# Splitting the first x load of a batched matmul into two transfers of half rows

## The chip, the cores and the metric

The kernel runs on one core of a Trainium2 chip. The metric is the device time of one execution in microseconds (us), taken as the median of several runs. All runs are "fast" (none is more than 1.5% above the fastest run of its kernel). A ratio of two kernels is the mean time of one kernel's fast runs over that of the other's of the same rounds, with a 95% interval, so it is not quite the ratio of the medians that are quoted beside it. "Same" means within 2%.

## The reference

```python
batch, m, k, n = 16, 512, 768, 1024        # float32 throughout
def reference(x, y):                       # x: (16, 768, 512), y: (16, 768, 1024)
    return np.einsum('bkm,bkn->bmn', x, y).astype(np.float32)
```

It is sixteen independent products. For each batch element 1.57 MB of x and 3.15 MB of y come in, and 2.10 MB go out. Together this is 109 MB.

## The kernel before

SyncE issues all transfers, in the order of the program. VectorE casts x and y to bf16, TensorE multiplies, and ScalarE copies PSUM to the output buffers. There are two buffers each for x and y in float32, two for each in bf16 and five for the output. A partition holds 6 neighbouring rows of k, so its part of x is one contiguous run of 12 KB in DRAM, and its part of y one of 24 KB.

The helper `wide_dma` on its first call with a key issues a plain transfer; every later call copies that instruction with a DRAM side whose rows are joined, four partitions' worth to a row for x and two for y. Both then read 48 KB at a time: the trace of the kernel before has 1440 packets of 49,152 bytes.

```python
def wide_dma(key, dst, src, dram_rows, load):
    if key not in made:
        made[key] = nc.sync.dma_start(dst, src)       # first call: plain
        return made[key]
    ...                                               # later calls: a copy with joined DRAM rows

def load(b):
    i = b % 2
    if b >= 2:
        nc.sync.wait_ge(cast, nx[b - 2])              # until the buffer of x is cast
    wide_dma("x", xs[i][:], x_v[b], 4, True).then_inc(sx[i], 16)
    if b >= 2:
        nc.sync.wait_ge(cast, nx[b - 2] + parts(b - 2))
    wide_dma("y", ys[i][:], y_v[b], 2, True).then_inc(sy[i], 16)
...
for b in range(B):                                    # VectorE
    i = b % 2
    n = 16 * (b // 2 + 1)
    if b >= 2:
        nc.vector.wait_ge(groups, 2 * (b - 1))
    nc.vector.wait_ge(sx[i], n)
    nc.vector.tensor_copy(xb[:, i], xs[i][:]).then_inc(cast, 1)
    nc.vector.wait_ge(sy[i], n)
    ...                                               # the cast of y
```

## Time and profile before

| what | before |
|---|---|
| time, median of the 3 runs | 260.69 us (260.46 to 260.75) |
| span of the profile | 259.0 us |
| busiest compute engine | PE, 69% |
| share of the 16 DMA engines on q1 | 98.5% |
| first cast of x, first cast of y | 7.14 us, 15.05 us |
| cast of the second y | 26.04 us |

The page is read from the DMA rows down, and not from the engines. A packet is one DMA record of the trace, and the page counts the share of the 16 DMA engines from these records. In the kernel before, queue q1 has 3744 packets of 12 to 48 KB, and 768 records of 4 bytes, which is 16 for each of the 48 transfers. These are called semaphore writes here, as the trace has just as many semaphore updates that came from transfers (768); the page counts them as packets too. The compute engines have gaps; the transfers have none to speak of but at the ends (in the DMA row, 7 tenths in the first slice, 5 in the last, and 8 or 9 in all others). The landings of the loads can be read at the casts that wait for them. The cast of y is the better mark of the two, as it always waits for its transfer in the first part of the kernel (the first seven end 3.6 to 6.1 us of idle time of VectorE, each released by the transfer).

### The profile page before, as it was taken

To read this page: it belongs to the slowest core of one execution; us is meant where nothing else is said; L and a number is where in the kernel's file an instruction comes from. 1 tells how busy PE (TensorE), PEld (TensorE's weight loads), DVE (VectorE), ACT (ScalarE), POOL (GpSimd) and SP (SyncE) were. 2 spreads that over 40 slices of the span, in tenths; PEclk is the share of its full clock that TensorE was granted. 3 is DMA by queue.
4 is the path that set the end of the run, shared out by engine and by line. 5 is a ranking of instruction groups with operands and counts; after the bars stand their busy time and mean duration, and the time that the engine had idled before them with its cause. 6 is when DMAs were issued, how large, how long until landed. Compare 5 with 4: busy or idle time off the path is not lost. (4 is left out here: it accounts for less than half of the span.)

```text
span 259.0 us, 2506 instructions
## 1 busy us (share of the span) xinstructions
PE 179.0 (69%) x768; PEld 88.9 (34%) x768; DVE 82.0 (32%) x33; ACT 60.9 (24%) x33; POOL 0.2 (0%) x4
## 2 busy tenths in 40 slices
PE   0009999999999006999069999595008999969500
PEld 0004555554545002454025555252003555534200
DVE  0261645527164350002245263300242536410000
ACT  1000342244220005222202241433000234052300
POOL 0000000000000000000000000000000000000000
PEclk9999999999999855899759999999555999988965
DMA  7999989899999999999999998999999999999995
GB/s 270 428 490 395 471 380 478 380 471 395 456 402 448 387 428 425 433 463 456 410 440 410 440 448 377 435 423 463 471 387 471 395 456 410 395 428 438 423 435 240
DMA packets 4514, 109.07 MB, mean 421 GB/s; under 512 B 768, under 2 KB 768, under 8 KB 768
## 3 DMA queue, kind: packets, MB, share of 16 engines
q1 hardware_dynamic: 4512, 109.05, 98.5%
q14 instruction: 2, 0.02, 0.0%
HBM read 75.50 MB, written 33.55 MB: 421 GB/s over the span
## 5 line engine op out<-in xcount | busy, mean ns | idle before, releaser
L154 PE MATMUL ps<-yb,xb 128*128 x768 | 179.0, 397 | 64.3 <-PEq L149 64.3
L154 PEld LDWEIGHTS ps<-yb,xb 128*128 x768 | 88.9, 116 | 154.0 <-issue 82.6
L170 ACT COPY ob<-ps 128x2048 f32<-128x2048 f32 x32 | 59.6, 1872 | 179.0 <-PE ps L154 139.9
L132 DVE CAST yb<-ys 128x6144 bf16<-128x6144 f32 (+1 forms) x17 | 53.8, 3171 | 77.2 <-DMA ys<-in_y_dram 77.2
L128 DVE CAST xb<-xs 128x3072 bf16<-128x3072 f32 x16 | 28.2, 1760 | 68.3 <-DMA xs<-in_x_dram 53.7
L170 ACT ACT_TABLE_LOAD x1 | 1.3, 1283 | 5.3 <-issue 5.3
L200 POOL MEMSET const-bfloat16-1.0<- 128x1 bf16 x1 | 0.1, 103 | 0.0
L200 POOL MEMSET const-uint8-127<- 128x1 uint8 x1 | 0.1, 103 | 0.0
L200 POOL MEMSET const-float32-0.0<- 128x1 f32 x1 | 0.1, 99 | 0.2 <-issue 0.2
L200 POOL MEMSET const-float32-1.0<- 128x1 f32 x1 | 0.1, 99 | 0.0
## 6 DMA issues: line engine op xcount, KB each, us to landing
ys<-in_y_dram SPq DMA_DIRECT2D x16, 3072.0 KB, 18.6
out_dram<-ob SPq DMA_DIRECT2D x16, 2048.0 KB, 26.3
xs<-in_x_dram SPq DMA_DIRECT2D x16, 1536.0 KB, 20.1
```

The source lines that it names most:

```text
L128: nc.vector.tensor_copy(xb[:, i], xs[i][:]).then_inc(cast, 1)
L132: nc.vector.tensor_copy(yb[:, i, ks], ys[i][:, ks]).then_inc(cast, 1)
L154: mm = nc.tensor.matmul(ps[g][:, m, nt], x_w[:, bass.ds(s, 1), kt, mo], yb[:, bass.ds(s, 1), kt, nt * NF:(nt + 1) * NF], start=(kt == 0), ...
L170: cp = nc.scalar.copy(ob[b % NO][:, g * HB:(g + 1) * HB].rearrange("p m (t f) -> p m t f", f=NF), ps[g][:])
L200: nc = _bacc.Bacc("TRN2", target_bir_lowering=False, num_devices=1)
```

## The change

The diff has no visible purpose but the start: the first x comes as two transfers, each of half of every partition's row, so that packets at the start are of 6 KB and not of 12. It asks for both halves before the cast.

```diff
+    XF = 2
...
-        wide_dma("x", xs[i][:], x_v[b], 4, True).then_inc(sx[i], 16)
+        if b == 0:
+            for k in range(0, KT, KT // XF):
+                ks = slice(k, k + KT // XF)
+                nc.sync.dma_start(xs[0][:, ks], x_v[0, :, ks]).then_inc(sx[0], 16)
+        else:
+            wide_dma("x", xs[i][:], x_v[b], 4, True).then_inc(sx[i], 16)
...
-        nc.vector.wait_ge(sx[i], n)
+        nc.vector.wait_ge(sx[i], n + 16 * (XF - 1) * (i == 0))
```

## The prediction

> **What bounds the kernel now.** I read the whole-program page first, then the time line of the start, then windows over single stretches of the transfers, then the waits of the DMA queue. From the page before:
>
> ```profile
> span 259.0 us, 2506 instructions
> PE 179.0 (69%) x768; PEld 88.9 (34%) x768; DVE 82.0 (32%) x33; ACT 60.9 (24%) x33; POOL 0.2 (0%) x4
> ...
> DMA  7999989899999999999999998999999999999995
> GB/s 270 428 490 395 471 380 478 380 471 395 456 402 448 387 428 425 433 463 456 410 440 410 440 448 377 435 423 463 471 387 471 395 456 410 395 428 438 423 435 240
> DMA packets 4514, 109.07 MB, mean 421 GB/s; under 512 B 768, under 2 KB 768, under 8 KB 768
> ...
> q1 hardware_dynamic: 4512, 109.05, 98.5%
> ```
>
> The reader is to see that no compute engine is above 69%, while the transfers hold the 16 DMA engines for 98.5% of the span and show a gap only in the first and the last slice. The bytes are fixed: 75.50 MB in and 33.55 MB out by the page. So this is a DMA-bound kernel, and a change can win time only by starting the stream of transfers earlier, by making its packets cheaper, or by shortening the tail after it. The chain of work that ended last names PE with only 5% of the span, because it breaks off at the last matmuls; I don't use it.
>
> The start, from the time line before (start, duration, engine, line, operation):
>
> ```profile
> 0.95 0.39 SPq L74 DMA_DIRECT2D xs<-in_x_dram  x1
> 1.39 0.42 SPq L74 DMA_DIRECT2D ys<-in_y_dram  x1
> 1.86 0.54 SPq L74 DMA_DIRECT2D xs<-in_x_dram  x1
> 2.44 0.65 SPq L74 DMA_DIRECT2D ys<-in_y_dram  x1
> 5.34 1.28 ACT L170 ACT_TABLE_LOAD   x1 [5.34 <-issue]
> 7.14 1.76 DVE L128 CAST xb<-xs 128x3072 bf16<-128x3072 f32 x1 [7.14 <-DMA xs<-in_x_dram]
> 8.93 0.47 SPq L74 DMA_DIRECT2D xs<-in_x_dram  x1
> 15.05 3.36 DVE L132 CAST yb<-ys 128x6144 bf16<-128x6144 f32 x1 [6.14 <-DMA ys<-in_y_dram]
> ```
>
> All four first loads are issued by 3.09 us. The first x is cast from 7.14 to 8.90 us, and then VectorE sits idle for 6.14 us until the first y lands at 15.05. TensorE needs both, so the landing of the first x has about 6 us of slack. An earlier or later first x alone is worth nothing.
>
> Windows over the start, in which the columns after the length are the busy time of five engines, the granted clock, the DMA share and the GB/s (a packet is counted with its whole time and size in the window in which it starts):
>
> ```profile
> 1.75:2.25 0.50, 0.00 (x0) 0.00 (x0) 0.00 (x0) 0.00 (x0) 0.00 (x0) 1.00 1.38 246
> 3.50:6.00 2.50, 0.00 (x0) 0.00 (x0) 0.00 (x0) 0.66 (x1) 0.00 (x0) 1.00 0.98 418
> 8.00:12.00 4.00, 0.00 (x0) 0.00 (x0) 0.90 (x1) 0.00 (x0) 0.00 (x0) 1.00 0.99 422
> 16.00:26.00 10.00, 7.01 (x23) 3.03 (x24) 4.17 (x2) 0.00 (x0) 0.00 (x0) 1.00 0.92 398
> 1.75:257.25 255.50, 178.96 (x768) 88.86 (x768) 81.99 (x33) 60.89 (x33) 0.00 (x0) 0.88 1.00 427
> ```
>
> The last line is the model I use: the stream begins at about 1.75 us, its last packets start by 257.25, and in between the engines' share is 1.00 at 427 GB/s. The other lines give the time of one packet, as share x length x 16 engines / number of packets, where the number is rate x length / packet size. First x, packets of 12,288 B: 0.98 x 2.5 x 16 = 39.2 us over 418 x 2.5 / 12.288 = 85 packets, 0.461 us each. First y, 24,576 B: 63.4 us over 68.7, 0.922 us. Later loads, 49,152 B: 147.2 us over 81.0, 1.818 us. Four packets of 12 KB cost 1.844 us where one of 48 KB costs 1.818, so each of the three additional packets costs about 0.009 us (estimate; the shares have two digits, so it may be 0 to 0.015). The very first packets: 1.38 x 0.5 x 16 = 11.0 us over 246 x 0.5 / 12.288 = 10 packets, 1.10 us each, which is 0.64 more than a packet in the stream.
>
> [...]
>
> **The change part by part.**
> 1. One more issue on the DMA queue, about 0.4 us by the rows above. The first y is then issued at about 1.8 instead of 1.39, the last of the first loads ends at about 3.5. The engines have the 1.57 MB of x to move until about 6.5 us, so the queue behind it is full in time. On the path: 0.
> 2. The first x: 128 packets of 12 KB become 256 of 6 KB, for each engine 16 instead of 8. The bytes are the same. Added: 8 x 0.009 = 0.07 us, all on the path, because the engines have no idle time to hide it in. One more semaphore write for each engine: about 0.01.
> 3. A part that the diff hides: the helper makes a plain transfer on the first call with each key, and copies it in its wide form afterwards. The first x no longer goes through the helper, so the second x is now its first call and comes plain: 12 KB packets instead of 48 KB, for each engine 8 packets instead of 2. Added: 6 x 0.009 = 0.05 us, on the path too.
> 4. The wait of the cast on both halves (32 instead of 16, and all later waits on that semaphore 16 higher) starts nothing early: no half is used alone. The order of instructions on every engine is otherwise the same, by a comparison of the two built programs. Time: 0.
> 5. The start of the stream. The first packets take 0.64 us more than the others. If this is latency alone, a shorter packet doesn't change when the second one flows: 0.
>
> Sum: 0.07 + 0.01 + 0.05 = 0.13 us longer, so 260.69 + 0.13 = 260.8 us. Nothing downstream amplifies it: by the waits of the DMA queue below, SyncE waits for casts for the buffers long before the queue runs dry, so a shift of 0.1 us shifts the stream and no more.
>
> ```profile
> SPq L74 <- DVE yb L132: 96.2, 12, 9.0
> SPq L74 <- DVE xb L128: 69.1, 12, 26.0
> ```
>
> **The rivals.** (a) A shorter ramp. [...]the first packet costs one packet's time extra, and with 6 KB this is 0.46 / 2 = 0.23 us less. For it speaks that 1.10 us is not far from twice 0.461 us; against it that one cannot tell it from plain latency. Net of the 0.13 us it makes 260.6 us. It may well be the intent of the change. (b) The transfers of half rows are dearer than I take them: the source of a half is 6 KB of every 12 KB, and the halves or the plain second x could leave the 16 engines more unequal, or the packets could be cut at 2 KB if the rows of the slice are not merged. Then an engine has 48 packets for the first x instead of 8, 40 x 0.009 = 0.36 us more, 261.1 to 261.2 us. Against it: in the kernel before only the 768 semaphore writes are under 8 KB, so the same three-dimensional form was merged to whole rows. (c) The earlier first half lets compute start early and the gain runs through: impossible here, since both halves are waited for and the first y lands some 6 us after the cast of x. This makes 0. (d) The phase between loads and TensorE changes, and a wait for buffers stops the stream. In the first phase a pair of loads takes 10.99 us, by the landings of y at 15.05 and 26.04, and a stop of a microsecond would need the queue to be several microseconds poorer than it is; I give it one chance in twenty and up to a microsecond either way.
>
> **Range and chances.** The sum is smaller than what repeated runs differ by (260.46 to 260.75), so the verdict can only be the same. Between (a) at 260.6 and (b) at 261.2 I add about 0.4 us on each side for the runs and (d): 260.2 to 261.5, centre 260.8. Two per cent is 5.2 us, forty times the sum; I give each side one chance in a hundred.
>
> **What would show it.** In the profile after: 4514 + 128 + 96 + 16 = 4754 packets; those under 8 KB 768 + 256 + 16 = 1040; a q1 share still at 98% or 99%; the first cast of x within 0.3 us of 7.14, that of y within 0.3 us of 15.05 and the second x as a plain load. If the start of the first y cast is earlier by some 0.2 us, and the span with it, rival (a) is right and step 5 is wrong. If there are some 512 packets more under 8 KB, the rows were not merged. A span that differs by over 1 us, or a slice in the middle with a DMA share of 7 or less that was not there before, would make the prediction wrong.

The 0.01 us of a semaphore write has no source in the prediction; the 768 records of 4 bytes in the trace of the kernel before have a median of 0.009 us. That the first packet costs one packet's time extra, in rival (a), is an assumption with the size of a measured packet (0.46 us).

## The result, and the profile after

The changed kernel took 260.68 us (260.51 to 260.75, 4 runs) against 260.72 us (260.46 to 260.76, 4 runs). The ratio is 1.000, with an interval from 0.9982 to 1.0017: "same". The output is correct.

The page of the changed kernel, with the rows that answer to those of before:

```profile
span 258.7 us, 2507 instructions
PE 176.9 (68%) x768; PEld 88.4 (34%) x768; DVE 82.0 (32%) x33; ACT 60.9 (24%) x33; POOL 0.2 (0%) x4
...
DMA  7999999999999999999999999999999999999996
DMA packets 4754, 109.07 MB, mean 422 GB/s; under 512 B 784, under 2 KB 784, under 8 KB 1040
...
q1 hardware_dynamic: 4752, 109.06, 98.6%
```

There is one instruction more, and 240 packets more. Those under 8 KB grew from 768 to 1040, which is the 256 packets of 6 KB and 16 semaphore writes. The DMA row is as full as before (q1 98.6%, before 98.5%).

The start of the changed kernel, from its time line (start, duration, engine, line, operation):

```profile
0.95 0.86 SPq L113 DMA_DIRECT2D xs<-in_x_dram  x2
1.86 0.43 SPq L75 DMA_DIRECT2D ys<-in_y_dram  x1
2.33 0.68 SPq L75 DMA_DIRECT2D xs<-in_x_dram  x1
3.05 0.53 SPq L75 DMA_DIRECT2D ys<-in_y_dram  x1
...
7.38 1.76 DVE L136 CAST xb<-xs 128x3072 bf16<-128x3072 f32 x1 [7.38 <-DMA xs<-in_x_dram]
...
14.99 3.36 DVE L140 CAST yb<-ys 128x6144 bf16<-128x6144 f32 x1 [5.85 <-DMA ys<-in_y_dram]
```

The two halves are issued back to back in 0.86 us, and the other three first loads move back by about half a microsecond. The first x lands 0.24 us later than in the profile of before, and the first y 0.06 us earlier. The cast of the first y still ends an idle time of VectorE of almost 6 us. The second y is cast at 25.98 us here and at 26.04 before. Whether the 0.24 us belongs to the change, only a second profile of the same kernel can tell; it is the first experiment.

### The profile page after: what moved, and what is told of

Same layout as the page of the kernel before. It is cut to its first block, busy times and chain, and to the rows that moved or that the text cites. A ratio compares the mean times of both kernels' runs of the same rounds, so it can differ in the third digit from the quotient of the medians.

```text
span 258.7 us, 2507 instructions
## 1 busy us (share of the span) xinstructions
PE 176.9 (68%) x768; PEld 88.4 (34%) x768; DVE 82.0 (32%) x33; ACT 60.9 (24%) x33; POOL 0.2 (0%) x4
## 2 busy tenths in 40 slices
DMA packets 4754, 109.07 MB, mean 422 GB/s; under 512 B 784, under 2 KB 784, under 8 KB 1040
## 3 DMA queue, kind: packets, MB, share of 16 engines
q1 hardware_dynamic: 4752, 109.06, 98.6%
## 5 line engine op out<-in xcount | busy, mean ns | idle before, releaser
L162 PE MATMUL ps<-yb,xb 128*128 x768 | 176.9, 394 | 65.7 <-PEq L157 65.7
```

Of the source, the lines that this page charges most:

```text
L162: mm = nc.tensor.matmul(ps[g][:, m, nt], x_w[:, bass.ds(s, 1), kt, mo], yb[:, bass.ds(s, 1), kt, nt * NF:(nt + 1) * NF], start=(kt == 0), ...
```

## The experiments

The theory is that the time is the start of the stream of transfers plus the sum of its packets, since the DMA engines never run dry (q1 has 98.5% of their time in the kernel before) and nothing downstream is on the path. The rivals are that smaller first packets shorten the ramp, that half rows are dear for the memory, and that an earlier or later start of compute runs through to the end.

### Both kernels once more

The edit is none.

> The kernel before once more, to learn what two profiles of one and the same kernel differ by. All theories: 260.7 us, ratio 1.000. The start of the stream (first packets), the first cast of x (7.14 us in the first profile) and that of y (15.05) should come back within 0.05 us if the changed kernel's later first x (7.38) is due to the change, and move by 0.1 to 0.3 us if it is the noise of one execution.

> The changed kernel once more, five rounds. Theory (a stream that is never empty, 0.009 us for each additional packet): 260.8 us, ratio about 1.0005. Rival (smaller first packets shorten the ramp by 0.23 us): 260.6 us, ratio about 0.9996. First cast of x at 7.38 again if its delay belongs to the change, first cast of y at 15.0.

In the same rounds the kernel before took 260.82 us (9 runs). Its copy took 260.81 us, ratio 0.9999 (0.9986 to 1.0013). The changed kernel took 260.80 us, ratio 0.9996 (0.9982 to 1.0009). The casts in the new profile of the kernel before:

```profile
7.54 1.76 DVE L128 CAST xb<-xs 128x3072 bf16<-128x3072 f32 x1 [7.54 <-DMA xs<-in_x_dram]
...
14.93 3.36 DVE L132 CAST yb<-ys 128x6144 bf16<-128x6144 f32 x1 [5.62 <-DMA ys<-in_y_dram]
```

One and the same kernel casts its first x at 7.14 in one execution and at 7.54 in another. The changed kernel's 7.38 (and 7.46 in its new profile) lies between, so its later first x says nothing about the change. The marks further on are steadier. The second y is cast at 26.04 and 25.93 us in the two profiles of before, and at 25.98 and 25.93 in the two of after. So the change is not seen at the second y within about 0.1 us. The added 0.13 us of the prediction is neither shown nor excluded by this.

### The halves alone, without the plain second x

```diff
         wide_dma("y", ys[i][:], y_v[b], 2, True).then_inc(sy[i], 16)
+        made.setdefault("x", made["y"])      # changed kernel, in load(): the second x is wide again
```

> The halves alone: the second x is given its wide form back (copied from the first y's instruction), which takes away the side effect of the change. Theory: 0.05 us less than the changed kernel, 260.75 us, 96 packets fewer than it (4658). Rival (the plain second x costs or saves more than its packets): differs from the changed kernel by over 0.3 us.

It took 260.76 us against 260.82 (ratio 0.9998, 0.9985 to 1.0012), and it has 4658 packets. The packet count confirms that the diff had changed the second x as a side effect. Its cost, 0.05 us by the prediction, is below what these runs can show. The rival asked for over 0.3 us between this kernel and the changed one; the medians are 0.04 us apart (260.76 and 260.80), and the means 0.08.

### The packets multiplied

```diff
# from the kernel before; 2 for x_halves_all, 6 for x_sixths_all
-        wide_dma("x", xs[i][:], x_v[b], 4, True).then_inc(sx[i], 16)
+        for k in range(0, KT, KT // 2):
+            ks = slice(k, k + KT // 2)
+            nc.sync.dma_start(xs[i][:, ks], x_v[b, :, ks]).then_inc(sx[i], 16)
...
-        nc.vector.wait_ge(sx[i], n)
+        nc.vector.wait_ge(sx[i], 2 * n)
```

> The suspected cost of packets multiplied: all 16 loads of x come as two transfers of half rows. Theory (0.009 us for each additional packet, all on the path): 14 packets more for each engine on 15 loads and 8 on the first, 218 x 0.009 = 1.96 us, and 16 semaphore writes, 0.14: 262.8 us, ratio 1.008. Rival (packets cost nothing, or are hidden behind the other traffic): 260.7 us. Rival (half rows are dear for the memory): over 264 us.

> As before, but all loads of x in six transfers of 2 KB for each partition. Theory: 46 packets more on 15 loads and 40 on the first, 730 x 0.009 = 6.6 us, and 80 semaphore writes, 0.7 us: 268.0 us, ratio 1.028. Rival (hidden): 260.7 us. Rival (half rows dear, or issue of transfers on SyncE as the bound): over 272 us, with holes in the DMA share.

All x in halves took 262.28 us against 260.79 (ratio 1.0052, 1.0038 to 1.0066). All x in sixths took 268.10 us against the same (ratio 1.0275, 1.0259 to 1.0290). The pages of the two, halves first:

```profile
DMA packets 8258, 109.07 MB, mean 419 GB/s; under 512 B 1024, under 2 KB 1024, under 8 KB 5120
...
q1 hardware_dynamic: 8256, 109.06, 98.8%
```

```profile
DMA packets 17475, 109.08 MB, mean 409 GB/s; under 512 B 2048, under 2 KB 2048, under 8 KB 14336
...
q1 hardware_dynamic: 17472, 109.06, 99.2%
```

The bytes are the same, the engines are as full as ever, and the rate over the span falls from 421 to 419 and to 409 GB/s. The halves add 218 data packets and 16 semaphore writes to each engine, so with all of the added time laid on them it is 1.49 us / 234 = 0.0064 us each (0.004 to 0.007 by the interval of the ratio). The sixths add 730 and 80, so 7.31 / 810 = 0.0090 us each (0.0083 to 0.0093). The rival that packets are hidden falls. So does the rival that half rows are dear: the halves cost less than the theory had for them.

There is a rival that I had not written down: a cost for each added transfer. It fits both runs with one figure, 1.49 / 16 = 0.093 us and 7.31 / 80 = 0.091 us, and these two totals can't refute it. The traces can, as they keep the size and the duration of each packet. Between the second and the seventh cast of y, the median packet of 6 KB took 0.238 us and that of 2 KB 0.087 us, where an eighth and a 24th of a 48 KB packet (1.829 us) are 0.229 and 0.076. So the surplus of about 0.01 us sits on the ordinary packet, and not on one in eight as it would if it belonged to the transfer. Less than this reaches the time: the records of packets that follow each other on an engine overlap by 0.003 to 0.004 us on average.

The same stretch shows the cost without the start and the end of the kernel. The second and the seventh cast of y in the kernel before, with halves and with sixths:

```profile
26.04 3.36 DVE L132 CAST yb<-ys 128x6144 bf16<-128x6144 f32 x1 [5.54 <-DMA ys<-in_y_dram]
...
81.01 3.36 DVE L132 CAST yb<-ys 128x6144 bf16<-128x6144 f32 x1 [5.47 <-DMA ys<-in_y_dram]
```

```profile
26.36 3.36 DVE L134 CAST yb<-ys 128x6144 bf16<-128x6144 f32 x1 [5.55 <-DMA ys<-in_y_dram]
...
81.70 3.36 DVE L134 CAST yb<-ys 128x6144 bf16<-128x6144 f32 x1 [5.48 <-DMA ys<-in_y_dram]
```

```profile
27.76 3.36 DVE L134 CAST yb<-ys 128x6144 bf16<-128x6144 f32 x1 [5.56 <-DMA ys<-in_y_dram]
...
84.61 3.36 DVE L134 CAST yb<-ys 128x6144 bf16<-128x6144 f32 x1 [5.49 <-DMA ys<-in_y_dram]
```

Five pairs of loads take 54.97, 55.34 and 56.85 us. So halves add 0.074 us to a pair, or 0.005 us for each of 15 added packets and semaphore writes, and sixths 0.376 us, or 0.0074 us for each of 51. The estimate of 0.009 us is too high for both. That the sixths came to 7.31 us in all, where the theory had 7.3, is thus partly luck: fifteen loads at 0.376 us make 5.6 us, and the rest came at the start and the end. The change's own 15 added packets and semaphore writes come to 0.07 us by the steady stretch and to 0.10 us by the whole run, instead of 0.13. Both figures are worked out from these runs; in the time of the changed kernel they can't be seen.

### An earlier or a later start

```diff
# y_first: the first y is issued before the first x
+        if b == 0:
+            wide_dma("y", ys[i][:], y_v[b], 2, True).then_inc(sy[i], 16)
         wide_dma("x", xs[i][:], x_v[b], 4, True).then_inc(sx[i], 16)
...
-        wide_dma("y", ys[i][:], y_v[b], 2, True).then_inc(sy[i], 16)
+        if b > 0:
+            wide_dma("y", ys[i][:], y_v[b], 2, True).then_inc(sy[i], 16)

# late_start: ahead of all transfers
+    for _ in range(24):
+        nc.gpsimd.sem_inc(late, 1)
+    nc.sync.wait_ge(late, 24)
```

> The first y is issued before the first x, so x lands last, at about 15 us; the cast of x then stands between its landing and that of y, and TensorE starts 1.76 us later, at about 20.7 instead of 18.99. Theory (the landing of the first x and the start of TensorE are off the path; the stream alone counts): 260.7 us, ratio 1.000, and TensorE has caught up by 75 us. Rival (an earlier start of compute runs through to the end): 262.4 us. Rival (ramp in proportion to the first packet, 24 KB instead of 12): 0.46 us more, 261.15 us.

> The first transfer is held back by 24 semaphore increments on GpSimd[...]. Theory: the end moves by as much as the first issue on SyncE does in the time line (0.95 us before), one for one, since the stream has no idle time to hide it in. Rival (slack elsewhere): less than half of the delay is seen in the time.

With y first the kernel took 260.86 us against 260.79 (ratio 1.0002, 0.9988 to 1.0015). Its time line of TensorE, with the length of one unbroken run of matmuls as the second number, and then that of the kernel before:

```profile
20.84 64.42 PE L157 MATMUL ps<-yb,xb 128*128 x288 [20.84 <-PEq L152]
```

```profile
18.99 43.72 PE L154 MATMUL ps<-yb,xb 128*128 x192 [18.99 <-PEq L149]
62.91 10.55 PE L154 MATMUL ps<-yb,xb 128*128 x48 [0.21 <-PEq L149]
```

TensorE starts 1.85 us later, and then works without a gap until 85.26 us, where the kernel before pauses for its loads from 62.71 us on. The delay is absorbed, and nothing of it reaches the end. I had written that it would catch up by 75 us. That was wrong: the kernel before finishes the same 288 matmuls at 84.46 us, so TensorE is still 0.80 us behind at 85.26, and it makes this good only in the pause that follows. In the kernel before this pause ends with ScalarE, which waited 21.76 us for a store and copied the next PSUM from 97.14 us on; both kernels go on at 99.2 to 99.3 us. The rival in which compute's start runs through (262.4 us) falls. The 0.46 us of the ramp rival, with packets of 24 KB at the start, lies just outside the interval too (0.15% of 260.8 is 0.39 us).

When all transfers are held back, it is different. The first issue in the time line of that kernel:

```profile
2.76 0.39 SPq L75 DMA_DIRECT2D xs<-in_x_dram  x1
```

It comes 1.81 us later than before, and the time is 262.60 us against 260.79 (ratio 1.0068, 1.0052 to 1.0083), which is also 1.81 us more. Here the start of the stream passes to the end one for one, 1.81 us of 1.81, while with y first the 1.85 us of compute's start don't show (ratio 1.0002). This is what the theory says. The second run delays compute too, but the first shows that a later compute alone cost nothing here.

### The first x in ever smaller pieces

```diff
# x0_sixths, from the changed kernel
-    XF = 2
+    XF = 6
```

> The same change taken further: the first x in six transfers of 2 KB for each partition. Theory: 40 packets more for each engine on the first x (0.36 us), 6 on the second (0.05), 5 more semaphore writes (0.05): 261.15 us. Rival (ramp in proportion to the first packet, 2 KB instead of 12): 0.38 us back, 260.8 us. A third way: six issues of 0.43 us make 2.6 us, and the queue runs dry at the start, with a DMA share under 0.9 between 3 and 6 us and over 261.5 us.

It took 261.69 us against 260.82 (ratio 1.0034, 1.0020 to 1.0047). That is 0.87 us more where the sum of packets gave 0.46, so half of it is not explained by the theory. The ramp rival, which wanted 260.8 us with first packets of 2 KB, is not borne out. The third way of the expectation is close: it asked for over 261.5 us, and for holes between 3 and 6 us. A window from 3 to 6 us, in which only packets of the first x start; the last two columns are the DMA share and the GB/s:

```profile
3.00:6.00 3.00, 0.00 (x0) 0.00 (x0) 0.00 (x0) 0.66 (x1) 0.00 (x0) 1.00 0.91 283
```

The first x moves at 283 GB/s here, where in the kernel before it moved at 418 (the window from 3.5 to 6 us in the prediction). The share has a hole of 9%. The packets take 0.91 x 3 x 16 = 43.7 us over 283 x 3 / 2.048 = 415 packets, 0.105 us each, while 2 KB by the bytes at 427 GB/s would take 2048 x 16 / 427,000 = 0.077 us, and 0.086 with the 0.009 us of a packet. So part of the loss is in holes and part in slow packets. By the packet records the slow ones are few: in this window the median is 0.084 us, and 6% of the packets took over one and a half times as long. (The profiled execution took 262.39 us, the slowest of the five, so its holes can't be set against the 0.87 us one for one.) Two further runs were to part the number of issues from the size of packets:

```diff
# x0_even_odd, from the changed kernel: still two transfers, but all packets of 2 KB
-            for k in range(0, KT, KT // XF):
-                ks = slice(k, k + KT // XF)
+            for k in range(XF):
+                ks = slice(k, KT, XF)

# x0_by_partitions: four transfers with packets of 12 KB (XF = 4)
+            for p in range(0, P, P // XF):
+                pq = slice(p, p + P // XF)
+                nc.sync.dma_start(xs[0][pq], x_v[0, pq]).then_inc(sx[0], 16)
```

> Six transfers of 2 KB pieces for the first x cost 0.87 us where the packets explain 0.46; this run parts the two things in it, small packets and many issues. The first x comes in two transfers, as in the change, but one takes the even and one the odd sixths of each row, so all its packets are of 2 KB. If the sum of packets is all (40 x 0.009 + 0.05 + 0.01): 261.2 us, and the rest of the cost of the sixths was the number of issues. If 2 KB packets are dearer in the first microseconds than later: 261.6 us, with the first y landing some 0.9 us later than at 15.0, as with the sixths.

> The other half of that question: four issues instead of two, with packets left at 12 KB, since each transfer takes 32 partitions of the first x whole. If the number of issues at the start costs (0.1 us for each of three more, by the sixths): 261.2 us. If not, only the plain second x and three semaphore writes count, 0.08 us: 260.9 us, and the first y lands at 15.0 to 15.1.

A window of the first of these, again one with packets of the first x alone:

```profile
3.00:5.00 2.00, 0.00 (x0) 0.00 (x0) 0.00 (x0) 0.00 (x0) 0.00 (x0) 1.00 0.96 286
```

The rate is as low as with the sixths, 286 GB/s. The even and odd sixths took 261.75 us against 260.81 (ratio 1.0039, 1.0025 to 1.0053), 0.94 us more where the packets explain 0.42. Two issues cost what six cost, but the traces show that they get there by different ways. The first issues of this kernel, and the stretch in which the kernel before already moved 246 GB/s (in the prediction):

```profile
0.95 1.30 SPq L113 DMA_DIRECT2D xs<-in_x_dram  x2
```

```profile
1.75:2.25 0.50, 0.00 (x0) 0.00 (x0) 0.00 (x0) 0.00 (x0) 0.00 (x0) 1.00 0.00 0
```

The first issue took 0.65 us instead of 0.39, and the first packet starts at 2.38 us instead of 1.97. The stream begins 0.41 us later, and by the theory this goes to the end one for one: 0.42 + 0.41 = 0.83 us, of 0.94 measured. So most of what I had put down to small packets at the start is a later start of the stream. With the sixths the first packet starts at 1.96 us, as before, but from 4 to 12 us the engines stood idle for 0.41 us on average, against 0.03 us in the kernel before and 0.07 us here. The number of issues is therefore not ruled out as a cause there, and what makes those holes stays open.

The first y landed at 16.68 us here, 1.6 us later than before, of which only 0.94 us reached the end. A landing follows the last of the transfer's 16 semaphore writes (in the kernel before, the first casts of x and of y and the second of y start 0.37 to 0.50 us after it). Those for the first y come 0.98 us later than before in the median, and the last of them 1.61 us later.

The transfers by partitions miss both of my expectations: 264.20 us against 260.81 (ratio 1.0131, 1.0115 to 1.0146), 3.4 us more. From 4 to 8 us of that kernel:

```profile
4.00:8.00 4.00, 0.00 (x0) 0.00 (x0) 0.00 (x0) 1.28 (x1) 0.00 (x0) 1.00 1.01 215
```

The engines are busy by the share (1.01), yet the stream moves at 215 GB/s, half of the usual 427. So it is the packets that took long: if all in this window are of 12 KB, 1.01 x 4 x 16 = 64.6 us over 215 x 4 / 12.288 = 70 packets make 0.92 us each (estimate), where the kernel before took 0.461 us by the same sum. What halves the rate of a transfer over 32 partitions is not shown by any run. This run can't tell what four issues cost, as this is buried under the halved rate. It does give the theory one more point: the first y is cast 3.48 us later (18.53 instead of 15.05), the second 3.48 us later (29.52 instead of 26.04), and the end moves by 3.4 us.

## Why the prediction was right

The time was forecast as 260.8 us in a range from 260.2 to 261.5, and 260.68 us were measured, and 260.80 us in the repetition. Point by point:

1. The additional issue was off the path, as forecast, as far as the time can show. It took 0.43 us, the first loads were all issued by 3.58 us, and the DMA row of the page has no new hole.
2. The packets of the first x: the counts were right to the last one (4754, and 1040 under 8 KB), so the rows were merged. The cost of a packet was the term that was mis-sized: 0.0064 us for packets of 6 KB by the run that has 4096 of them, and 0.005 in its steady stretch, where the sum had 0.009. That the 0.009 came near is partly luck. It was read from shares of two digits; the packet records of the same trace have medians of 0.460 us at 12 KB, 0.912 at 24 KB and 1.829 at 48 KB, which makes 2 x 0.460 - 0.912 = 0.008 us from the first two and (4 x 0.460 - 1.829) / 3 = 0.004 us from the pair that was used.
3. The plain second x was there, and it was worth less than can be measured, as forecast.
4. The wait on both halves starts nothing early. The run with y first shows that a start of TensorE 1.85 us later costs nothing. That an earlier one, by a cleverer wait, would win nothing either is to be expected from this, but no run shows it.
5. The start of the stream was taken as unchanged by the packet's size. That holds as far as the time goes. Rival (a) missed with y first, narrowly, and with the sixths, where another cost could have hidden its gain. The packet records speak against it too: from the first packet to 4 us an engine stood idle for 0.30 and 0.68 us on average in the two profiles of before, and for 0.38 and 0.21 us in the two of after, so one kernel alone varies by more than the rival's 0.23 us. The reason given in the prediction, latency alone, was not tested by itself.

The sum of the parts is thus 0.07 to 0.10 instead of 0.13 us by the multiplied runs, and the time of the changed kernel (0.9996 with 0.9982 to 1.0009) is compatible with it and with zero. A forecast of no change at all would have been as good in the number. What was shown is the frame: a stream that never runs dry, with its start and its packets on the path and everything else off it. Rival (b) was wrong for halves. One step further, 2 KB pieces of the first x cost twice their packets; in the one run most of the rest is a later first packet, in the other it is open.

## What to carry to other kernels

Where the trace shows the DMA engines busy from start to end (98.5% here), look first whether a change alters the number of bytes, the number of packets, the moment at which the first packet flows or the rate of a stretch. Here 240 more packets were not seen in the time (ratio 0.9996), while 12,960 more cost 7.31 us, a first issue 1.81 us later cost 1.81 us, and a first x at 215 GB/s cost 3.4 us. A first x that landed at 15.24 instead of 7.14 us, with y first, cost nothing that could be measured. Multiply a suspected small cost until it stands out of the noise (here sixteen-fold), since one application of it can't be measured. And when a helper treats its first call differently, a diff that goes round the helper changes the next call too.
